# One table of places for every 4 and 8 KB buffer, whole 8 KB runs of expert weights, and a reordered last pair of experts

## The chip, the cores and the metric

The kernel runs on 1 core of one Trainium2 chip. The metric is the device time in microseconds. Before the change it is 823.57 us, the median of 3 runs (818.97 to 824.45). The profiled execution took 820.36 us, of which the span of recorded instructions is 818.6 us; all rows below are of that one execution. From run to run the kernel moves by about 0.7%, so a change of less than 1% can hardly be told from none here.

## The reference

One layer over 256 latent tokens of width 1024, with 256 context tokens, all in fp32. Cut to what matters:

```python
sh1, sc1, g1, sh2, sc2, g2 = split(silu(c) @ w_mod + b_mod, 6)      # and the same for the context
h, hc = modulate(x, sh1, sc1), modulate(ctx, sh1c, sc1c)
u, q, k, v, gates = split(h @ w_in);  uc, _, kc, vc, _ = split(hc @ w_in)
y_ssm = s5_both_directions(u, states left by uc)                    # scan of 64 states per group
o     = attention(rope(rms(q)), [rope(rms(k)), rms(kc)], [v, vc])   # 8 heads, 2 kv heads
g     = gelu(y_ssm)
mix   = (sig(gate_ssm) * (g @ w_glu_a) * sig(g @ w_glu_b) + sig(gate_attn) * (o @ w_attn_o)) @ w_out
x     = layer_norm(2**.25 * x + g1 * mix) * ln1_g + ln1_b
# 32 experts: best group of 4, best 2 of its 8 experts, for each token
y     = sum over chosen e of  w[t, e] * ((silu(m @ w_gate[e]) * (m @ w_up[e])) @ w_down[e]),  m = modulate(x, sh2, sc2)
x     = layer_norm(2**.25 * x + g2 * y) * ln2_g + ln2_b
```

The 32 experts' three matrices (gate and up 1024x512, down 512x1024) are 6 MB for an expert and 192 MB in all; every one is read once.

## The kernel before

**Two stages.** The first ("the flow", up to about 350 us) is everything up to the router. Its work is cut into some 45 small streams (Python generators), and a list of numbers, `Flow.ORDER`, says which stream emits its next piece; so the order of instructions on every engine is fixed when the kernel is built. The second stage loops over 16 pairs of experts (`for p in range(NP)`). Almost every instruction is recorded through one helper, line 238, so rows are told apart by tile names.

**A pair of experts.** Up to 64 tokens of each of two experts are gathered into one 128-wide operand. TensorE (PE) runs gate, 64-row products `gu<-ew,x` over eight k of 128 for both experts; after the first CB = 4 k of gate come eight products `acc<-yh,cw` and `acc<-yl,cw` that bring the pair before back to its tokens (`combine`). Then up, also eight k. ACT takes the silu of gate, DVE multiplies it with up into `hh`, PE transposes `hh` in between the gathering of the next pair (`dispatch`, `turn`), DVE copies it to `hT`, and the 32 products `y<-ew,hT` are down. In the last pair there is nothing to gather, so PE idles while `hh` and `hT` are made. The split of a result into two fp32r parts, `yh` (ACT) and `yl` (DVE), is what `combine` multiplies with `cw`.

**Buffers.** Large buffers come from several pools: `raw` (3 of 8 KB a partition), `p8` (5 of 8 KB), `p4` (15 of 4 KB), and `w`, `l4`, `g4` (4 of 4 KB each). The flow's own weights pass through `raw`, `l4`, `g4` and the rest. As the flow frees them, expert weights (`ew`) are loaded into them ahead of time (`prefetch8`, `prefetch4`, `refill`), and in the second stage the same buffers, 38 places of 4 KB as the list `first` has them, are used in a ring (`ring_tile`).

**Expert loads.** `eload` issues them on SP's queue. A buffer of 8 KB takes four k, one transfer of 1 MB in which each partition reads 8 KB in one run; a buffer of 4 KB takes two k, a transfer of 512 KB with runs of 4 KB. SP works its list in order: a transfer that waits for its buffer holds every later one. A transfer also waits, on one of eight semaphores (`DMAHW0` to `DMAHW7`) taken in turn, until the transfer eight before it has landed.

**Two pieces in the middle of the second stage.** `overflow()` handles tokens beyond 64 for an expert. It reads a count from memory on every engine (line 1709) and branches on it (line 1719); with these inputs there are none, so the body is skipped. It stands ahead of pair 8 (`OVP`). The last layer norm's gain and bias, one row of 1024 each, are spread over the partitions by four products of a 1-row operand, `y<-ew,count 1*128`, with an ACT copy each, in pair 14 ahead of up.

**Three transfers of the flow that the prediction speaks of.** `tm<-kscr` is eight loads of 128 KB on SP, of tables that PE reads as `ss<-tm,U`. `yT<-yscr` is one load of 512 KB that ACT issues on its own queue, in rows of 1 KB; ACT then works it into `gTh`, which PE reads in `acc<-wh,gTh`. `g<-in_w_mod` are loads of modulation weights in groups of four.

Of the kernel before, what the change touches and what calls it, by code (L numbers as in the profile page):

```python
# [31 lines left out]
NRAW = 3  # L32
N8, N4, N2, NPE = 5, 15, 6, 5
# [52 lines left out]
class Flow:  # L86
# [95 lines left out]
    def note(self, key, op, args, kw):  # L182
# [6 lines left out]
        for a in aps:  # L189
            assert a.tensor.name not in self.dead, (op, a.tensor.name)  # L190
# [1755 lines left out]
```

## Time and profile before

| | us |
|---|---|
| runs | 818.97, 823.57, 824.45 |
| profiled execution | 820.36 |
| its span | 818.6 |
| PE busy in the span | 765.9 (94%) |
| DVE busy | 371.6 (45%) |
| ACT busy | 295.3 (36%) |
| SP's DMA queue, share of the 16 engines' time | 83.7%, 265.29 MB |

PE's busy share is an average over two different stages. In the flow PE, DVE and ACT are all busy and the DMA engines between 45 and 93% (in stretches of 25 us). In the second stage DVE and ACT are at about a fifth, PE is at 100% of most 50 us stretches, and at the same time the DMA engines are at 1.02 of their time: two limits side by side. Times of rows are microseconds from the start of the span. A mean for one instruction is in ns. "idle before <-releaser" in brackets is how long the engine stood still ahead of a row and what ended that.

### The profile page before, as it was taken

Reading aid. Unit: us, or ns where it says so; the run is one execution under the profiler, and the core shown is the slowest. Engines: PE = TensorE matmul, PEld = TensorE weight load, DVE = VectorE, ACT = ScalarE, POOL = GpSimd, SP = SyncE. Lnnn points to the kernel's source line nnn. Section 1 sums busy time; section 2 is a strip of 40 time slices with the busy share of each in tenths; the row PEclk is TensorE's granted clock in tenths of the full one; section 3 lists DMA queues with packets and bytes.
Section 4 is the critical chain, followed back from the end, with each engine's and each line's share of the span. In section 5 each row is a group of like instructions: output and inputs, shape, how many; then the busy total and the mean of one; then the engine's idle time right before and its main releaser. Section 6 shows DMA issues by size and latency. Waiting matters only on the chain. (4 is left out here: it accounts for less than half of the span.)

```text
span 818.6 us, 11438 instructions
## 1 busy us (share of the span) xinstructions
PE 765.9 (94%) x4371; PEld 437.5 (53%) x4371; DVE 371.6 (45%) x857; ACT 295.3 (36%) x574; POOL 30.8 (4%) x48
## 2 busy tenths in 40 slices
PE   3999989989999999899999999999999999999994
PEld 1787777646667787644443444344344534444431
DVE  7999969877544767813211221122122122202115
ACT  5553586756988544522210221022022102202200
POOL 0004202000000000200000000000000000000000
PEclk9899999999999999899999999999999999999997
DMA  9977275593658686989999999999999999999992
GB/s 359 349 307 279 52 238 147 216 323 106 192 144 309 249 292 219 348 329 399 414 412 413 412 414 413 412 413 412 411 413 412 411 414 412 413 413 409 412 408 84
DMA packets 71138, 269.73 MB, mean 330 GB/s; under 512 B 12195, under 2 KB 17699, under 8 KB 59173
## 3 DMA queue, kind: packets, MB, share of 16 engines
q1 hardware_dynamic: 65268, 265.29, 83.7%
q0 software_dynamic: 1152, 2.59, 1.1%
q10 hardware_dynamic: 4656, 1.05, 0.6%
q8 instruction: 37, 0.61, 0.3%
q14 instruction: 25, 0.20, 0.1%
HBM read 265.79 MB, written 3.11 MB: 329 GB/s over the span
## 5 line engine op out<-in xcount | busy, mean ns | idle before, releaser
L238 PE MATMUL gu<-ew,x 128*64 128x512 f32 x1024 | 233.0, 602 | 4.4 <-PEq L1719 2.5
L238 PEld LDWEIGHTS gu<-ew,x 128*64 128x64 f32 x1024 | 75.3, 138 | 149.7 <-issue 134.5
L238 PE MATMUL y<-ew,hT 128*64 128x512 f32 x512 | 113.5, 595 | 0.8 <-DVE hT L238 0.8
L238 DVE TENSOR_TENSOR hh<-hh,gu 128x512 f32<-128x512 f32 x16 | 11.0, 688 | 212.1 <-PE gu L238 212.1
L238 ACT ACTIVATE x<-y,modT 128x128 f32<-128x128 f32 x120 | 45.1, 455 | 139.4 <-PE y L238 139.4
L238 DVE TENSOR_TENSOR wl<-raw,wh 128x1024 fp32r<-128x1024 f32 x52 | 63.4, 1223 | 28.7 <-ACT wh L238 28.5
L238 PEld LDWEIGHTS y<-ew,hT 128*64 128x64 f32 x512 | 36.3, 137 | 66.7 <-issue 63.6
L238 ACT ACTIVATE wh<-raw 128x1024 fp32r<-128x1024 f32 x52 | 54.9, 1059 | 25.2 <-PE acc L238 24.9
L238 PEld LDWEIGHTS y<-d,xh 128*128 128x128 f32 x480 | 55.9, 192 | 12.2 <-issue 10.5
L238 PE MATMUL acc<-wh,hh 128*128 128x512 f32 x128 | 57.3, 448 | 3.1 <-DVE q L238 2.0
L238 PE MATMUL y<-d,xh 128*128 128x128 f32 x480 | 60.0, 278 | 0.0
L238 ACT ACTIVATE yh<-x 128x512 fp32r<-128x512 f32 x32 | 20.1, 629 | 105.0 <-DVE x L238 105.0
L238 DVE SCALAR_TENSOR_TENSOR x<-y,wsl,g 128x512 f32<-128x512 f32 x32 | 24.0, 751 | 66.7 <-PE y L238 66.7
L238 ACT ACTIVATE hh<-gu 128x512 f32<-128x512 f32 x16 | 9.6, 597 | 123.4 <-PE gu L238 123.4
L238 PE MATMUL acc<-wh,hl 128*128 128x512 f32 x128 | 51.4, 401 | 0.0
L238 PE MATMUL acc<-wl,hh 128*128 128x512 f32 x128 | 51.3, 401 | 0.0
L238 DVE TENSOR_TENSOR yl<-x,yh 128x512 fp32r<-128x512 f32 x32 | 22.2, 692 | 24.1 <-ACT yh L238 24.1
L238 PEld LDWEIGHTS acc<-wh,hh 128*128 128x128 f32 x128 | 24.4, 190 | 11.8 <-issue 4.3
L238 PEld LDWEIGHTS acc<-wh,hl 128*128 128x128 f32 x128 | 24.5, 191 | 5.9
L238 PEld LDWEIGHTS acc<-wl,hh 128*128 128x128 f32 x128 | 24.5, 192 | 5.7 <-issue 1.2
L238 PE MATMUL acc<-yh,cw 128*128 128x512 f32 x64 | 27.0, 422 | 0.4 <-ACT yh L238 0.4
L238 PE MATMUL acc<-yl,cw 128*128 128x512 f32 x64 | 25.3, 395 | 0.2 <-DVE yl L238 0.2
(263 smaller groups left out, 1052.8 us busy)
## 6 DMA issues: line engine op xcount, KB each, us to landing
ew<-in_w_exp_gate_dram SPq DMA_DIRECT2D x92, 512.0 KB, 11.7
ew<-in_w_exp_up_dram SPq DMA_DIRECT2D x88, 512.0 KB, 11.4
ew<-in_w_exp_down_dram SPq DMA_DIRECT2D x84, 512.0 KB, 11.4
ew<-in_w_exp_down_dram SPq DMA_DIRECT2D x21, 1024.0 KB, 12.6
ew<-in_w_exp_up_dram SPq DMA_DIRECT2D x20, 1024.0 KB, 12.6
ew<-in_w_exp_gate_dram SPq DMA_DIRECT2D x18, 1024.0 KB, 12.5
g<-in_w_mod_dram SPq DMA_DIRECT2D x32, 512.0 KB, 6.7
raw<-in_w_in_dram SPq DMA_DIRECT2D x14, 1024.0 KB, 5.7
```

The source lines that it names most:

```text
L238: return f(*args, **kw)
```

## The change

**Places.** All the pools named above become one pool of 45 places of 4 KB, held as pairs (tiles `b0` to `b22`, 8 KB each but the last). Which place a buffer of the flow gets is read from a table, `Flow.PLACE`, in the order in which the buffers are made. The room for the two more places comes from `dynamic_dma_scratch_size=8192`. Rows of order show `b7_2709` where they showed `raw_2878` or `ew_2992`. `g2` now shares the place of `g1`.

**Expert loads.** `eload` now always loads four k, 1 MB in runs of 8 KB. The flow loads 18 of them where it loaded 16 MB, with a new stream `refill("x4", 4)`; twenty pairs of places (`units`) go round in the second stage. A pair is given back when all four k in it have been multiplied (`weight`), and `reload()` is called after gate, after up and after down.

**The last pair.** `overflow()` moves from pair 8 to the last pair, behind up. Three of the four products that spread the last norm's rows move from pair 14 into the last pair's up, behind six of its eight k (`UB` is 6, was 4); the fourth goes behind the last products of all. In the last pair `hh` is multiplied, transposed and copied in two halves of 256 columns. The second half of the last result is no longer split: two plain fp32 products take the place of four fp32r ones.

```diff
-    for n_, b_ in (("p8", N8), ("p4", N4), ("p2", N2), ("pe", NPE), ("t2", 2)):
+    for n_, b_ in (("p2", N2), ("pe", NPE), ("t2", 2)):
...
+    def places(self, at, n, dt=FT):
+
+        s, k = at // 2, FR if dt == FR else FT
+        if self.held.get(s, (None, None))[1] != k:
+            b = self.area.tile([P, min(2, NS - 2 * s) * W4], k, tag=f"b{s}", name=f"b{s}", bufs=1)
...
-                kn = 2 if small_ else 4
...
+        small_ = KINDS[tag][1] == 1
+        w, e, k0 = etiles[e_n[0]]
+        e_n[0] += 1
+        at = fl.at[fl.name(new(tag, [P, 2 if small_ else 4, F], name="ew"))]
+        if small_:
+            at = min(at, fl.at[fl.name(new(tag, [P, 2, F], name="ew"))])
+        r = fl.places(at, 2 * W4).rearrange("p (k c) -> p k c", c=F)
+        erun(r, w, e, k0, 4)
...
+    def reload():
+        while rest and units:
...
+    def weight(w, e, k):
+        u = where.pop((w, e, k))
+        left[u] -= 1
+        if not left[u]:
+            units.append(u)
+        return eready.pop((w, e, k))
...
-    NP, OVP, CB, UB = NE // 2, 8, 4, 4
+    NP, CB, UB = NE // 2, 4, 6
...
-        if p == OVP:
-            overflow()
...
         into(p, 1, range(UB))
+        if not more:
+            for i in range(3):
+                lnp = ln2_row(i, gu_p if i == 2 else y_p)
         into(p, 1, range(UB, KT))
...
+            overflow(lnp)
+            halves = [slice(256 * z, 256 * z + 256) for z in range(2)]
+            for c_ in halves:
+                tt(hh[:, c_], hh[:, c_], pgs[1][:, c_], OP.mult)
...
+            if more or n == 0:
+                split(yb[:, n], yh[n], yl[n])
+                if not more:
+                    combine(cw, (n,), True)
+            else:
+                for a in range(2):
+                    T.matmul(acc[a][n], cw[:, a].bitcast(FT), yb[:, n], start=False, stop=True)
+                ln2_row(3, gu_p)
```

In `ORDER` two entries 45 (the new stream) are put in and one 37 is moved.

**The order, first place: SP, the last two groups of `w_mod` loads** (about 166 to 175 us). Before:

```order
L238 DMA g4_1957<-in_w_mod_dram 128x1024 [waits DMAHW1_49,PE_49]
L238 DMA g4_1959<-in_w_mod_dram 128x1024 [waits DMAHW2_49,PE_49]
L238 DMA g4_1961<-in_w_mod_dram 128x1024 [waits DMAHW7_49,DMAHW3_49,PE_49]
L238 DMA g4_1963<-in_w_mod_dram 128x1024 [waits DMAHW4_49,DMAHW0_49,PE_49]
L238 DMA g4_2030<-in_w_mod_dram 128x1024 [waits DMAHW5_49,PE_49]
L238 DMA g4_2032<-in_w_mod_dram 128x1024 [waits DMAHW6_49,PE_49]
L238 DMA g4_2034<-in_w_mod_dram 128x1024 [waits DMAHW7_49,PE_49]
L238 DMA g4_2036<-in_w_mod_dram 128x1024 [waits DMAHW0_49,PE_49]
```

Now:

```order
L273 DMA b2_107<-in_w_mod_dram 128x1024 [waits DMAHW5_49]
L273 DMA b13_882<-in_w_mod_dram 128x1024 [waits DMAHW1_49,PE_49]
L273 DMA b10_481<-in_w_mod_dram 128x1024 [waits DMAHW7_49,DMAHW2_49,PE_49]
L273 DMA b9_113<-in_w_mod_dram 128x1024 [waits DMAHW3_49,DMAHW0_49,PE_49]
L273 DMA b12_123<-in_w_mod_dram 128x1024 [waits DVE_49]
L273 DMA b2_107<-in_w_mod_dram 128x1024 [waits DMAHW5_49,PE_49]
L273 DMA b13_882<-in_w_mod_dram 128x1024 [waits DMAHW6_49,PE_49]
L273 DMA b10_481<-in_w_mod_dram 128x1024 [waits DMAHW7_49,DMAHW4_49,PE_49]
```

The first load of each group no longer waits for PE's last use of its buffer.

**Second place: SP, from the `tm` loads to the second half of `w_glu_b`** (about 215 to 249 us). Before:

```order
L238 DMA raw_2538<-in_w_glu_b_dram 128x2048 [waits DMAHW6_49,DMAHW1_49,DVE_49]
L238 DMA ew_2592<-in_w_exp_gate_dram 128x2048 [waits DMAHW2_49]
L238 DMA tm_2601<-kscr_92 16x16x128 [waits DMAHW3_49,Activation_49]
L238 DMA tm_2601<-kscr_92 16x16x128 x2
L238 DMA tm_2601<-kscr_92 16x16x128 [waits DMAHW7_49]
L238 DMA tm_2601<-kscr_92 16x16x128 [waits DMAHW0_49]
L238 DMA tm_2601<-kscr_92 16x16x128 [waits DMAHW1_49]
L238 DMA tm_2601<-kscr_92 16x16x128 [waits DMAHW2_49]
L238 DMA tm_2601<-kscr_92 16x16x128 [waits DMAHW3_49]
L238 DMA ew_2690<-in_w_exp_gate_dram 128x2048 [waits DMAHW4_49,PE_49,Activation_49]
L238 DMA raw_2755<-in_w_glu_a_dram 128x2048 [waits DMAHW5_49,DVE_49]
L238 DMA raw_2878<-in_w_glu_b_dram 128x2048 [waits DMAHW0_49,DVE_49]
```

Now:

```order
L273 DMA b0_1347<-in_w_exp_gate_dram 128x2048 [waits DMAHW6_49,DMAHW2_49,DVE_49]
L273 DMA b21_1165<-kscr_89 16x16x128 [waits DMAHW3_49,PE_49]
L273 DMA b21_1165<-kscr_89 16x16x128 [waits DMAHW5_49]
L273 DMA b21_1165<-kscr_89 16x16x128
L273 DMA b21_1165<-kscr_89 16x16x128 [waits DMAHW7_49]
L273 DMA b21_1165<-kscr_89 16x16x128 [waits DMAHW0_49]
L273 DMA b21_1165<-kscr_89 16x16x128 [waits DMAHW1_49]
L273 DMA b21_1165<-kscr_89 16x16x128 [waits DMAHW2_49]
L273 DMA b21_1165<-kscr_89 16x16x128 [waits DMAHW3_49]
L273 DMA b1_115<-in_w_exp_gate_dram 128x2048 [waits DMAHW4_49,PE_49,Activation_49]
L273 DMA b11_337<-in_w_glu_a_dram 128x2048 [waits DMAHW5_49,PE_49]
L273 DMA b7_2709<-in_w_glu_b_dram 128x2048 [waits DMAHW7_49,DVE_49,PE_49]
```

The first `tm` load now waits for PE, which reads the older `tm` in the same place, where it waited for ACT. The `w_glu_b` load waits for a product of PE (of a `wh` in `b7`) where it waited for a DVE split. Three small loads and three expert loads of 1 MB follow it, where six of 512 KB did.

**Third place: PE, the end of the last pair's up.** Before, from its last products on:

```order
L238 MATMUL gu<-ew,x_3166 64x512 [waits DMAHW5_49]
L238 MATMUL gu<-ew,x_3166 64x512 x2
L238 MATMUL gu<-cst,hh 128x128 [waits DVE_49]
L238 MATMUL gu<-cst,hh 128x128 x3
L238 MATMUL y<-ew,hT 64x512 [waits DMAHW6_49,DVE_49]
```

Now, from the first use of the last two up transfers on (`b7` and `b8`):

```order
L273 MATMUL gu<-b_2709,b_452 64x512 [waits DMAHW3_49]
L273 MATMUL gu<-b_1212,b_452 64x512 [waits DMAHW4_49]
L273 MATMUL gu<-b_2709,b_452 64x512
L273 MATMUL gu<-b_1212,b_452 64x512
L273 MATMUL y<-b_1347,count 128x512 [waits PE_49] x2
L273 MATMUL gu<-b_1347,count 128x512 [waits Activation_49]
L273 MATMUL gu<-b_2709,b_452 64x512
L273 MATMUL gu<-b_1212,b_452 64x512
L273 MATMUL gu<-b_2709,b_452 64x512
L273 MATMUL gu<-b_1212,b_452 64x512
L1759 TENSOR_LOAD total [waits DVE_49]
L1769 COMPARE_AND_BRANCH
```

The three row products and the branch stand behind the wait for the last up transfers; the two transposes of each half follow the branch.

## Rows read from the trace of the kernel before

**Rows 1.** Windows of 50 us; last column GB/s, before it DMA share, granted clock.

```profile
400.00:450.00 50.00, 50.00 (x249) 20.91 (x250) 10.18 (x18) 8.22 (x18) 0.00 (x0) 1.00 1.02 413
700.00:750.00 50.00, 48.67 (x246) 23.03 (x243) 11.56 (x20) 9.13 (x21) 0.00 (x0) 1.00 1.02 411
```

**Rows 2.** Timeline of PE: start, length, what, idle before.

```profile
407.60 3.60 PE L238 MATMUL gu<-ew,x 128*64 128x512 f32 x16
...
574.60 5.35 PE L238 MATMUL gu<-ew,x 128*64 128x512 f32 x16 [2.52 <-PEq L1719]
...
685.81 3.60 PE L238 MATMUL gu<-ew,x 128*64 128x512 f32 x16
...
754.11 3.79 PE L238 MATMUL y<-ew,count 1*128 1x512 f32 x8
757.82 8.78 PE L238 MATMUL gu<-ew,x 128*64 128x512 f32 x32
...
777.88 3.60 PE L238 MATMUL gu<-ew,x 128*64 128x512 f32 x16
...
783.46 10.72 PE L238 MATMUL gu<-ew,x 128*64 128x512 f32 x48
...
796.47 7.24 PE L238 MATMUL y<-ew,hT 128*64 128x512 f32 x32 [0.79 <-DVE hT L238]
```

**Rows 3.** A window of 4 us behind the branch; granted clock third from the end.

```profile
574.00:578.00 4.00, 3.40 (x9) 1.23 (x11) 0.35 (x1) 0.00 (x0) 0.00 (x0) 0.59 1.01 416
```

**Rows 4.** Window at the end of the load stream.

```profile
801.00:802.00 1.00, 1.00 (x7) 0.66 (x5) 0.32 (x1) 0.63 (x1) 0.00 (x0) 1.00 0.08 31
```

**Rows 5.** Gate's expert loads on the page: count, KB each, us to landing.

```profile
ew<-in_w_exp_gate_dram SPq DMA_DIRECT2D x92, 512.0 KB, 11.7
...
ew<-in_w_exp_gate_dram SPq DMA_DIRECT2D x18, 1024.0 KB, 12.5
```

**Rows 6.** DMA view of three windows: 648:656, 456:460 and 552:556.

```profile
DMA packets 899, 3.28 MB, mean 410 GB/s; under 512 B 99, under 2 KB 99, under 8 KB 899
...
DMA packets 245, 1.69 MB, mean 422 GB/s; under 512 B 28, under 2 KB 28, under 8 KB 50
...
DMA packets 257, 1.71 MB, mean 427 GB/s; under 512 B 29, under 2 KB 29, under 8 KB 68
```

**Rows 7.** Timeline of ACT and DVE behind the last down product.

```profile
804.59 0.63 ACT L238 ACTIVATE yh<-x 128x512 fp32r<-128x512 f32 x1 [2.95 <-DVE x L238]
805.26 0.69 DVE L238 TENSOR_TENSOR yl<-x,yh 128x512 fp32r<-128x512 f32 x1 [0.76 <-ACT yh L238]
```

**Rows 8.** PE's waits, 160 to 200 us: total, times, longest.

```profile
PE ss L238 <- DMA g<-in_w_mod_dram: 3.4, 5, 1.1
```

**Rows 9.** Timelines of SP, PE and ACT around the `tm` and `yT` loads.

```profile
218.25 5.27 SPq L238 DMA_DIRECT2D tm<-kscr  x8
...
224.92 0.43 PE L238 MATMUL ss<-tm,U 128*32 128x128 f32 x8
...
233.71 0.43 PE L238 MATMUL ss<-tm,U 128*32 128x128 f32 x8
...
248.53 0.33 SPq L238 DMA_DIRECT2D raw<-in_w_glu_b_dram  x1
...
253.21 1.06 ACT L238 ACTIVATE gTh<-yT 128x1024 fp32r<-128x1024 f32 x1
...
255.62 0.48 PE L238 MATMUL acc<-wh,gTh 128*128 128x512 f32 x1
```

**Rows 10.** Loads on other queues: `tm` and `yT`, `kscr` at 70:82, `kscr` at 95:102.

```profile
DMA to landing us min/median/max: 4.9/5.1/5.3
...
yT<-yscr ACTq DMA_DIRECT2D x1, 512.0 KB, 4.0
...
kscr<-kall POOLq DMA_DIRECT2D x4, 32.0 KB, 5.7
...
kscr<-kall POOLq DMA_DIRECT2D x4, 32.0 KB, 2.1
```

More of the change, by code (lines that the diff above doesn't have):

```diff
@@ L254, in start @@
         aps = aps or ()
-        if any(a.tensor.name not in self.done for a in aps):
+        if any(self.name(a) not in self.done for a in aps):
             return None
@@ L1310, in flow_tile, with erun, eplace @@
-    def flow_tile(tag, shape):
-        return new(tag, shape, name="ew")
+    EW = ("w_exp_gate", "w_exp_up", "w_exp_down")
+    etiles = [(w, e, k0) for p in range(2) for w in EW for k0 in (0, 4) for e in (2 * p, 2 * p + 1)][:18]
+    eready, where, left, e_n = {}, {}, {}, [0]
+    def erun(o, w, e, k0, kn):
+        SY.dma_start(o.rearrange("p k c -> p (k c)"),
+             bass.AP(tensor=I[w].tensor, offset=I[w].offset + (e * P * 8 + k0) * F, ap=[[8 * F, P], [1, kn * F]]))
+    def eplace(o, w, e, k0, kn, at):
+        for k in range(kn):
+            eready[w, e, k0 + k] = o[:, k]
+            where[w, e, k0 + k] = at // 2
+        left[at // 2] = left.get(at // 2, 0) + kn
@@ L1323, in prefetch8 @@
     def prefetch8():
-        for _ in range(N8 - 3):
-            yield ask("Z", None, None, lambda: e_n[0] >= 4 and room("p8", 1)(), p8=1)
-            eload("p8", flow_tile)
+        for _ in range(2):
+            yield ask("Z", None, None, lambda: e_n[0] >= 2 and room("p8", 1)(), p8=1)
+            eload("p8")
         yield ask("Z", None, None, room("p8", 1), p8=1)
@@ L1352, in prefetch4 @@
     def prefetch4():
-        for i in range((N4 - 4) // 2):
+        for i in range(5):
             yield ask("Z", None, None, room("p4", 2), p4=2)
-            eload("p4", flow_tile)
+            eload("p4")
             if i == 2:
@@ L1618, in chunks @@
         while len(out_) < n:
-            tag = first[ring_n[0] % len(first)]
-            ring_n[0] += 1
-            m = 1 if small_(tag) else 2
-            r = ring_tile(tag, [P, m, D])
-            out_ += [r[:, z] for z in range(m)]
-        return out_
+            r = unit(D)[1]
+            out_ += [r[:, z] for z in range(2)]
+        return out_[:n]
     def weights():
@@ L1716, in overflow @@
         y = y.rearrange("p (n c) -> p n c", n=2)
-        pg = [gu_p.tile([P, F], FT, name="gu") for _ in range(2)]
-        yp = [y_p.tile([P, 512], FT, name="y") for _ in range(2)]
+        hh = t2[:, 8 * CAP:]
+        yp = pg = [y_p.tile([P, F], FT, name="y") for _ in range(2)]
         with tc.If(rv > 0):
@@ L1798, in into, with ln2_row @@
             for e in range(2):
-                T.matmul(pgs[i][64 * e:64 * e + 64], xgb[:, k, 64 * e:64 * e + 64], eready.pop((w, 2 * p + e, k)),
+                T.matmul(pgs[i][64 * e:64 * e + 64], xgb[:, k, 64 * e:64 * e + 64], weight(w, 2 * p + e, k),
                          start=(k == 0), stop=(k == KT - 1), tile_position=(0, 64 * e))
-    RING = sum(1 if small_(t_) else 2 for t_ in first)
+    def ln2_row(i, pool_):
+        row = eready["ln2", i // 2][:, F * (i % 2):F * (i % 2) + F]
+        ps = pool_.tile([P, F], FT, name="y" if pool_ is y_p else "gu")
+        T.matmul(ps, count[0:1, 0], row[0:1], start=True, stop=True)
+        S.activation(row, ps, AF.Copy)
+        return ps
+    reload()
     for p in range(NP):
@@ L1829, in build @@
             weighted(p + 1)
[L1830 to L1836 removed]
         into(p, 1, range(UB))
+        if not more:
+            for i in range(3):
+                lnp = ln2_row(i, gu_p if i == 2 else y_p)
         into(p, 1, range(UB, KT))
[L1839 to L1840 removed]
+        reload()
         hT = hTb
```

168 lines of the change are left out of this document (87 added, 81 removed).

## The prediction

> **What bounds the kernel now.** I read the 50 us windows first, then PE's timeline of the second stage, then the DMA view, and last the waits in the flow. The windows show two limits at once: from 400 us on PE is busy in 50.00 or 48.67 of 50 us, and the DMA engines are at 1.02 of their time with 411 to 413 GB/s [rows 1]. So each limit gets its own sum, and the later one counts.
>
> PE's chain: the first gate products of pairs stand at 407.60 and, ten pairs later, at 685.81 [rows 2]. Of these 278.2 us one pair had the branch: 2.52 us idle, and then 16 products in 5.35 us where other pairs need 3.60, together 4.3 us. The rest is 27.4 us a pair. From 685.81 to 777.88, three pairs, it is 92.1 us, 9.9 more than 3 x 27.4. Of that 3.8 us are the eight one-row products, and the 32 up products behind them took 8.78 us, 1.6 more than two thirds of the 10.72 that 48 of them took in the last pair [rows 2]. The remaining 4.5 us are late weights and small differences.
>
> The load stream: a pair's weights are 12 MB, 12.58 million bytes, which at 412.5 GB/s take 30.5 us. That is more than PE's 27.4, so what was loaded ahead is eaten up pair by pair. The last byte comes just ahead of 802, where the DMA share has fallen to 0.08 [rows 4], while PE is still in its last 32 products, from 796.47 for 7.24 us [rows 2]. Hence PE without its 14 us of losses would have run into the stream: what the stream gives is the question.
>
> **The change, part by part.**
>
> *Longer runs.* Gate's loads are 92 of 512 KB and 18 of 1 MB [rows 5], 28% of the bytes in 8 KB runs; up and down are alike. A window with no packet of 8 KB moved 410 GB/s, two that are nearly all 8 KB moved 422 and 427 [rows 6]. From the mean, 412.5 = 1/(0.72/410 + 0.28/x), x is 419. I take 420, near the low end, as the long stretch has more bytes than windows of 4 us. The stream is full from about 386 on, and the last up transfer lands the last 4 MB earlier than 802, at 802 - 10.2 = 791.8. Those 406 us become shorter by 1 - 412.5/420 = 1.8%, which is 7.2 us. Bounds: 0 (410, no gain) to 14 (427).
>
> The Trainium skill, "DMA: Bandwidth & Descriptors", section "Why small descriptors are slow", speaks against so much: it names three cycles of 32 bytes and 32 bytes of metadata a descriptor and finds merging worth it only at 256 bytes or less. By that, as an estimate, 8 KB runs are some 1.5% better than 4 KB ones, 1.0% of the mixed stream, 4.1 us, and the sum below would be 3.1 us worse. The rows show 3 to 4%, so I hold to them.
>
> *A megabyte more goes round*, 20 where there were 19: the stream is ahead by one transfer, 2.5 us at 412.5 GB/s. A place now comes free after four k instead of two, which can take back 1.8 us (16 products of 3.60 us are four k, half of it two). I take 2.5; bounds 0.7 and 2.5.
>
> So the last up transfer lands at 791.8 - 7.2 - 2.5 = **782.1**.
>
> *PE's chain to the same point.* Pair 15's gate would start at 777.88 - 4.3 (branch) - 5.4 (rows and slow products behind them) - 4.5 (late weights) = 763.7, and the fifth k of up, which needs the last up transfers, is 3.6 + 2.0 (combine: 783.46 - 777.88 - 3.6) + 3.6 + 3.6 = 12.8 later: 776.5 [rows 2]. So PE waits for the stream, about 5.6 us spread over the last pairs; most of what the branch and the rows cost in the middle is not gained, since those 14 us were covered by a stream that was late anyway.
>
> *Behind the last up transfer* all is on the path: 16 products 3.6, the three rows moved there 2.8 (three quarters of 3.79), the branch 2.5 (its idle time at pair 8), transposes and copies in halves, of which about 0.8 is not under the branch, and 32 products 7.1. Together 16.8, so the last down product ends at 798.9. Before it ended at 803.7: **-4.8**. The down transfers land until 782.1 + 10.0 = 792.1 and are in time. On DVE and ACT the branch comes long before `hh` is wanted; it costs nothing while they idle there, and 5 to 6 us if they were late.
>
> *The last result unsplit.* ACT's 0.63 and DVE's 0.69 us [rows 7] leave the path, and two plain products replace four: **-1.4**, bounds -1.6 and -0.5. The fourth row's product and copy are used only at the end of the first half's norm, several us later, and lie beside DVE's work.
>
> *The flow.* Three terms.
> First, the `w_mod` loads: PE waited 3.4 us for them in five places [rows 8], always for a late one of four; two of three groups now start one load early. I take -2.0, bounds -3.4 and 0.
> Second, `tm`: its first load was issued at 218.25, and must now wait for the end of the last reading of the older table, 224.92 + 0.43; that is 7.1 us later. The eight took 5.27 us to issue and 5.1 to land [rows 9, 10], so the last comes at about 235.4 or, if the landing is shorter with an emptier queue, 233.6. PE wants it at 233.71. I take +1.0, bounds 0 and 1.7.
> Third, `yT`: it landed in 4.0 us with its queue's engines to itself, as `w_glu_b` was issued only at 248.53 [rows 9, 10]. Now `w_glu_b` waits for a PE product that ends some 2 us earlier, so 1 MB, two small transfers and three more MB run beside it. A load on another queue does suffer: the 32 KB ones took 5.7 us beside a full queue and 2.1 in an empty one [rows 10]. `gTh` was ready at 253.21 + 1.06 = 254.27, and PE took it at 255.62, so 1.35 us are free. I take a delay of 2.3, +1.0 net; bounds 0 and the third rival's 8.6.
> The flow's sum is 0. A slip of it moves PE and stream alike, since the ring is refilled as pair 0 frees places.
>
> The sum: -4.8 - 1.4 + 0 = **-6.2 us**. The profiled execution of 820.36 becomes 814.2. It lies 3.2 under the median of the runs, so the median becomes 823.57 - 6.2 = **817.4**. Changes of 1% (815.3 and 831.8) are about what a measurement here tells from none.
>
> **Rivals.**
>
> 1. *The stream is no limit any more* (chance 0.25). At 427 GB/s the last up transfer lands at 791.8 - 13.8 - 2.5 = 775.5, before PE's 776.5. Then the down products end at 776.5 + 16.8 = 793.3, -10.4, with the tail -11.8, and 811.8; with the `w_mod` gain in full and no slip, 809. For it: the two windows of 422 and 427. Against it: both are 4 us long.
>
> 2. *Runs of 8 KB give next to nothing* (0.13). The stream gains only the megabyte, the last up transfer lands at 789.3, the down products end at 806.1, and with the tail it is +1.0: 824.6. Against it: [rows 6]. By the page of the Trainium skill named above, 4.1 us of the 7.2 would come and the time be 820.5, between this and the forecast.
>
> 3. *The flow slips, and the kernel is slower* (0.13). The two queues take turns, one packet each. `yT` is 512 rows of 1 KB, 32 on each of 16 engines; if each waits for a run of 8 KB, 8192 x 16 bytes at 422 GB/s or 0.31 us, it takes 9.9 us longer, 8.6 over what is free. PE standing still so long may also be followed by a lower clock, as the window after the branch shows 0.59, near the lower of 1.2 and 2.4 GHz [rows 3], which cost 1.75 us there. That makes 823.57 - 6.2 - 1.0 + 8.6 + 1.75 = 826.7. It decides from a slip of 6 us on. For it: the 32 KB loads. Against it: the small transfers behind `w_glu_b` have rows of 1 KB too and let `yT` through quickly.
>
> The rest, 0.49, is the forecast; inside it the clock may fall after the branch as it did in pair 8, +1.75, so 819.2.
>
> **How the numbers follow.** Faster by over 1% is rival 1 and a small part of the forecast: 0.32. Slower by over 1% needs rival 3 with something beside it, or a stall that no row shows: 0.09. The rest, 0.59, is within 1%. The likeliest time is 817.4. The range reaches to rival 1 without its full flow gain, 810.5, and up to rivals 2 and 3 in part, 825.5.
>
> **What would show it.** In the new profile: windows of 50 us at 419 to 422 GB/s with DMA share above 1; PE's `gu` waiting for expert loads in the last four or five pairs, 4 to 7 us in all; no idle time at pair 8 and no one-row products in pair 14; last-pair up products broken by a wait, then three rows, then about 2.5 us idle named after the branch; the first down product at about 791.5; about 1.4 us less from there on. In the flow, no waits for `g<-in_w_mod`, `tm` landing at 234 to 235, `yT` in 6 us or so. The forecast is wrong if the windows show 412 or 427, if `yT` takes 10 us, or if PE is late in the flow for a reason that none of these terms has.

## The result

| | before | after |
|---|---|---|
| median, us | 822.13 (818.97 to 824.45, 4 runs) | 810.05 (808.71 to 813.46, 4 runs) |
| ratio of times, with 95% interval | | 0.9867 (0.9844 to 0.9890) |
| profiled execution, its span | 820.36, 818.6 | 813.46, 811.6 |
| start of the second pair's gate, from the span's start | 380.16 | 379.70 |
| from there to the span's end ("second stage" below) | 438.4 | 431.9 |

Faster by 1.3%, where 0.75% was forecast. The profiled execution took 813.46; the forecast for it was 814.2. The four runs spread over 4.8 us, and the profiled one is the slowest of them. The unaltered change was timed twice more, beside other kernels, at ratios of 0.9921 (0.9899 to 0.9944) and 0.9890 (0.9863 to 0.9917). The mean of the three is 0.989, some 8.8 us.

**The load stream.** Windows of 50 us of the profile after, with the columns of [rows 1]:

```profile
400.00:450.00 50.00, 50.00 (x249) 20.57 (x247) 10.18 (x18) 8.23 (x18) 0.00 (x0) 1.00 1.01 421
700.00:750.00 50.00, 49.86 (x244) 21.27 (x242) 10.21 (x19) 8.70 (x20) 0.00 (x0) 1.00 1.01 421
```

DMA share is above 1 as before, and the stream moves 421 GB/s in place of 413 and 411. The page lists the gate loads in one form now, 64 of 1 MB, in place of the two of [rows 5]:

```profile
b<-in_w_exp_gate_dram SPq DMA_DIRECT2D x64, 1024.0 KB, 19.8
```

**PE in the last two pairs.** Timeline of PE of the profile after; it answers to [rows 2]:

```profile
736.73 3.65 PE L273 MATMUL gu<-b,b 128*64 128x512 f32 x16
...
742.34 7.98 PE L273 MATMUL gu<-b,b 128*64 128x512 f32 x34
751.64 3.65 PE L273 MATMUL gu<-b,b 128*64 128x512 f32 x14 [1.32 <-DMA b<-in_w_exp_up_dram]
...
766.56 3.64 PE L273 MATMUL gu<-b,b 128*64 128x512 f32 x16
...
772.17 7.97 PE L273 MATMUL gu<-b,b 128*64 128x512 f32 x34
781.45 1.93 PE L273 MATMUL gu<-b,b 128*64 128x512 f32 x6 [1.31 <-DMA b<-in_w_exp_up_dram]
783.31 1.98 PE L273 MATMUL y<-b,count 1*128 1x512 f32 x4
785.13 1.31 PE L273 MATMUL gu<-b,count 1*128 1x512 f32 x2
786.38 3.29 PE L273 MATMUL gu<-b,b 128*64 128x512 f32 x8
790.35 0.41 PE L273 MATMUL y<-cst,hh 128*128 128x128 f32 x2 [0.69 <-DVE hh L273]
790.68 0.41 PE L273 MATMUL gu<-cst,hh 128*128 128x128 f32 x2
791.32 7.09 PE L273 MATMUL y<-b,hT 128*64 128x512 f32 x32 [0.23 <-issue]
```

PE waits for an up transfer in pair 14 and in pair 15, 1.3 us each time; the view of waits has 2.6 us in two places for 350 to 815. That is less than PE loses. One of these products takes 0.59 us, and the next one starts some 0.21 us after it; so PE's row shows a stall only from the end of the product that is still running, and a short stall not at all. PE's weight loads (PEld) do not overlap in that way. Their view of waits, from 380 us on:

```profile
PEld gu L273 <- DMA b<-in_w_exp_up_dram: 6.8, 5, 2.2
```

The five places lie in pairs 13, 14 and 15, and some 0.3 us of each is the usual gap between weight loads. The pair times agree: from gate to gate pairs 2 to 12 take 27.36 or 27.37 us, pair 13 takes 28.58 and pair 14 29.83 (736.73 to 766.56), so 1.2 and 2.5 us are lost; in pair 15 another 2.1 are, since the 34 products ahead of 781.45 take 9.28 us where an unbroken row of them takes 7.18 (48 take 10.52). Together PE loses 5.8 us to the stream.

The first down product is at 791.32 (forecast 791.5), the last ends at 798.41 (forecast 798.9; before 803.71). The branch causes no idle time: behind it PE waits 0.69 us for DVE's `hh`. But the last eight up products, behind the three rows, took 3.29 us. The window there, granted clock third from the end:

```profile
785.00:790.00 5.00, 4.66 (x11) 0.95 (x9) 0.21 (x1) 1.26 (x3) 0.00 (x0) 0.66 0.82 318
```

0.66 over 5 us is a stretch partly at the lower of the two levels, 1.2 GHz, after the six one-row products; in the 3.3 us of the eight products alone it is 0.58.

**The tail.** Timeline of DVE of the profile after, behind the last down product:

```profile
798.46 0.75 DVE L273 SCALAR_TENSOR_TENSOR b<-y,wsl,b 128x512 f32<-128x512 f32 x1 [1.24 <-PE y L273]
799.12 2.00 DVE L273 BATCH_NORM_STATS2 fst<-acc 128x6 f32<-128x512 f32 x3
```

The ACT and DVE steps of [rows 7] are gone from this place. From the end of the last scaling to the end of the statistics it is 1.91 us (801.12 - 799.21), where it was 3.26 (807.76 - 804.50) in these rows of before:

```profile
803.75 0.75 DVE L238 SCALAR_TENSOR_TENSOR x<-y,wsl,g 128x512 f32<-128x512 f32 x1 [1.38 <-PE y L238]
...
805.87 1.89 DVE L238 BATCH_NORM_STATS2 fst<-acc 128x6 f32<-128x512 f32 x3
```

**The flow.** PE's waits in 160 to 200 us of the profile after (it answers to [rows 8]):

```profile
PE ss L273 <- DMA b<-in_w_mod_dram: 2.3, 3, 1.1
```

The timelines of SP, PE and ACT that answer to [rows 9]; `tm` and `yT` are called `b` too:

```profile
222.45 6.06 SPq L273 DMA_DIRECT2D b<-kscr  x8
...
232.46 0.86 PE L273 MATMUL ss<-b,b 128*32 128x128 f32 x24 [1.66 <-DMA b<-kscr]
...
244.69 0.37 ACTq L273 DMA_DIRECT2D b<-yscr  x1
...
245.12 0.33 SPq L273 DMA_DIRECT2D b<-in_w_glu_b_dram  x1
```

And the landing of `yT` in the DMA view of 240:250, as in [rows 10]:

```profile
b<-yscr ACTq DMA_DIRECT2D x1, 512.0 KB, 4.0
```

`w_glu_b` is issued 0.43 us behind `yT`, and `yT` lands in 4.0 us all the same. PE waits 1.66 us for `tm`. Between ACT's table loads at 154.65 and 185.77 before lay 31.1 us, in which [rows 8] lie; now they are at 156.48 and 184.60, 28.1 us apart.

### The profile page after: what moved, and what is told of

It reads as the page before. It is cut to its first block, busy times and chain, and to the rows that moved or that the text cites. A ratio compares the mean times of both kernels' runs of the same rounds, so it can differ in the third digit from the quotient of the medians.

```text
span 811.6 us, 11217 instructions
## 1 busy us (share of the span) xinstructions
PE 762.1 (94%) x4371; PEld 435.6 (54%) x4371; DVE 370.8 (46%) x858; ACT 294.2 (36%) x573; POOL 30.9 (4%) x48
## 5 line engine op out<-in xcount | busy, mean ns | idle before, releaser
L273 PE MATMUL gu<-b,b 128*64 128x512 f32 x1024 | 231.0, 597 | 3.4 <-DMA b<-in_w_exp_up_dram 2.6
L273 PE MATMUL acc<-b,b 128*128 128x512 f32 (+1 forms) x792 | 202.4, 390 | 4.4 <-DVE q L273 2.0
L273 PEld LDWEIGHTS acc<-b,b 128*128 128x128 f32 x792 | 136.5, 190 | 36.2 <-issue 9.2
L273 PEld LDWEIGHTS gu<-b,b 128*64 128x64 f32 x1024 | 73.3, 137 | 148.3 <-issue 138.6
L273 PE MATMUL y<-b,hT 128*64 128x512 f32 x512 | 113.4, 595 | 0.2 <-issue 0.2
L273 ACT ACTIVATE b<-y,modT 128x128 f32<-128x128 f32 x120 | 45.2, 456 | 138.5 <-PE y L273 138.5
L273 DVE TENSOR_TENSOR b<-b,b 128x1024 fp32r<-128x1024 f32 (+1 forms) x61 | 72.0, 1187 | 30.8 <-ACT b L273 29.7
L273 ACT ACTIVATE b<-b 128x1024 fp32r<-128x1024 f32 (+3 forms) x70 | 71.3, 1028 | 26.5 <-PE acc L273 24.2
L273 PEld LDWEIGHTS y<-d,b 128*128 128x128 f32 x480 | 55.9, 192 | 12.2 <-issue 11.4
L273 PE MATMUL y<-d,b 128*128 128x128 f32 x480 | 60.0, 278 | 0.0
L273 ACT ACTIVATE yh<-b 128x512 fp32r<-128x512 f32 x31 | 19.5, 629 | 97.5 <-DVE b L273 97.5
```

The lines of the kernel that those rows point to most:

```text
L273: return f(*args, **kw)
```

## The experiments

All times below of a "second stage" run from the second pair's gate to the span's end of the one profiled execution; "PE's wait" is the sum of waits for up transfers in PE's rows, "weight loads" the same in the rows of PEld, which also show the short ones (with some 0.3 us of usual gap in each). The stage is the finer gauge: three profiles of the unaltered change have 431.9, 431.6 and 431.8, two of before 438.4 and 438.7, while the start of the stage moves between 377.1 and 382.6 from run to run in kernels whose flow is the same.

| kernel | median, us | ratio (95%) | second stage | PE's wait | weight loads |
|---|---|---|---|---|---|
| again | 813.63 | 0.9921 (0.9899 to 0.9944) | 431.6 | 2.6 | 6.6 |
| run4k | 823.51 | 1.0040 (1.0022 to 1.0057) | 443.4 | 7.6 | 20.9 |
| ring19 | 815.33 | 0.9937 (0.9912 to 0.9962) | 432.2 | 4.2 | 9.2 |
| half64 | 1175.08 | (not given) | 790.8 | 97.5 | (not used) |
| nobranch | 815.31 | 0.9906 (0.9873 to 0.9939) | 431.5 | 3.4 | 7.9 |
| rows14 | 812.91 | 0.9883 (0.9851 to 0.9914) | 431.5 | 0 | 1.7 |
| both | 815.01 | 0.9918 (0.9890 to 0.9946) | 434.2 | 0 | 0.7 |
| resplit | 814.64 | 0.9910 (0.9879 to 0.9940) | 433.8 | 2.6 | 6.6 |
| again2 | 812.92 | 0.9890 (0.9863 to 0.9917) | 431.8 | 2.6 | 6.9 |
| rows14nb | 809.81 | 0.9843 (0.9814 to 0.9872) | 428.5 | 1.0 | 2.8 |
| rowsmid | 810.23 | 0.9866 (0.9834 to 0.9898) | 430.7 | 1.6 | 4.5 |

The lines from again to half64 ran on one chip, from nobranch to resplit on another, the last three on a third. The kernel before had 820.63, 821.67 and 821.90 there.

### The longer runs: run4k, half64, and the change again

**again**: the change, unaltered.

> The changed kernel unaltered, for a second trace and a closer ratio. The forecast put the change at -6.2 us (ratio 0.9925); the first timing said 0.987, -11 us, while its one profiled execution was -6.9 us against the one of before. If the forecast's sum is right for the second stage and the profiled execution merely began badly, this trace has the second stage as in the first one (last up products behind a wait for the stream of 1 to 3 us, last down product near 8 us ahead of the DVE end) and differs in the flow, by 2 to 5 us: PE's waits for w_mod in the first 60 us near 0.8 instead of 2.7, a half-speed stretch more or less. The rival: the second stage itself varies by 3 to 5 us.

Measured: 813.63 against 820.63. Its profile repeats that of the change to 0.3 us from the second gate on; its flow is 2.6 us shorter (gate at 377.06). Of these 1.8 lie where it was expected: PE's waits for `w_mod` in the first 60 us are 0.9, where the change's first profile has 2.7.

**run4k**: two k a transfer everywhere, 4 KB runs, all else as changed.

```diff
-            n = 1 if w == "w_exp_down" and k0 and e == NE - 1 else 4
+            n = 1 if w == "w_exp_down" and k0 and e == NE - 1 else 2
```

> The changed kernel with each 1 MB transfer of the second stage issued as two of 512 KB with runs of 4 KB a partition, same places and order; the 18 transfers of the flow stay as they are. Stream theory (8 KB runs shorten a stream that sets the end): 50 us windows fall from 420 to 410 GB/s, PE's waits for expert loads grow from 2.6 to about 10 us, time +7 to +10 us, ratio to before 0.995 to 1.0. Rival (the stream is no limit; the moved pieces made the gain): windows fall too, but the time stays within 2 us of the changed kernel, ratio 0.985 to 0.989.

Measured: 9.9 us slower than again, and 0.4% slower than before. A 50 us window of run4k:

```profile
450.00:500.00 50.00, 50.00 (x264) 22.82 (x264) 10.97 (x20) 9.73 (x22) 0.00 (x0) 1.00 1.03 409
```

Its DMA view of 600:620:

```profile
DMA packets 2240, 8.17 MB, mean 408 GB/s; under 512 B 249, under 2 KB 249, under 8 KB 2239
```

And that of the same stretch of the profile after:

```profile
DMA packets 1156, 8.43 MB, mean 422 GB/s; under 512 B 128, under 2 KB 128, under 8 KB 128
```

At a full DMA share 409 became 421 GB/s, 2.9%. Of the some 406 us in which the stream is full that is nearly 12 us; the second stage differs by 443.4 - 431.6 = 11.8. So the rate sets the time nearly one for one, which it could not if the stream were no limit. The pair times show how: in both kernels a pair takes 27.4 us while the loads that went ahead last; from pair 11 on run4k's pairs take 29.1 to 31.7 us, where again has 28.4 and 29.8 in pairs 13 and 14 only. run4k is also 5.0 us longer in the second stage than before the change. But it has no 8 KB runs there, where 28% of the expert bytes had them before: at 409 in place of 412.5 GB/s the 406 us become some 3.5 longer. So the run shows that the rest of the change gains nothing without the faster stream; that it would lose with the old mix of runs is not shown.

**half64**: 8 KB runs in transfers of 512 KB, each of 64 partitions, to part the run's length from the transfer's size.

```diff
-                erun(r[:, k:k + n], w, e, k0 + k, n)
+                for h in (0, 64) if n == 4 else ():
+                    SY.dma_start(r[h:h + 64].rearrange("p k c -> p (k c)"),
+                         bass.AP(..., offset=I[w].offset + ((e * P + h) * 8 + k0) * F, ap=[[8 * F, 64], [1, 4 * F]]))
```

> The changed kernel with each 1 MB transfer of the second stage issued as two of 512 KB, 64 partitions each, runs of 8 KB kept. If the length of the run makes the rate, windows stay at 420 GB/s and the time within 2 us of the changed kernel. If it is the size of the transfer, windows fall to 410 to 412 and the time grows by 7 to 10 us.

Measured: 1175.08 us. It did not part the two, since transfers of half as many partitions moved nearly half as much. A 50 us window of half64, and its DMA view of 600:620:

```profile
600.00:650.00 50.00, 36.06 (x130) 14.36 (x132) 4.34 (x8) 3.96 (x10) 0.00 (x0) 0.83 1.02 227
```

```profile
DMA packets 688, 4.51 MB, mean 225 GB/s; under 512 B 139, under 2 KB 139, under 8 KB 139
```

The DMA share is 1.02, the rate 227 GB/s. Whether the run's 8 KB or the transfer's 1 MB gives the 2.9% stays open: in all other kernels here the two change together.

### One place less: ring19

```diff
+    spare = units.pop()
```

> The changed kernel with one pair of places fewer in the second stage (19 go round, as many bytes as before the change). Stream theory: the stream is one transfer less ahead, 2.5 us later at the last up products, so +2.5 us (1 to 3). Rival (the extra megabyte is not needed, PE sets the end): 0 to +0.5 us.

Measured: the wait in the last pair's up ends 403.61 us after the second gate (780.91 - 377.30); in again it is 401.58 (778.64 - 377.06). One megabyte in the ring is worth 2.0 us there, where the forecast took 2.5. By the rows of PE's weight loads the waits grew by 2.6 us. The second stage lost only 0.6, which is close to what the rival had foreseen (0 to 0.5), but for another reason: the eight products behind the rows ran at the full clock this time, 1.94 us at a granted clock of 1.00, and not 3.41 as in again. The median is 1.7 us higher. PE of ring19:

```profile
780.91 1.93 PE L273 MATMUL gu<-b,b 128*64 128x512 f32 x6 [1.31 <-DMA b<-in_w_exp_up_dram]
...
785.54 1.94 PE L273 MATMUL gu<-b,b 128*64 128x512 f32 x8
```

### The branch and the rows: nobranch, rows14, both, rows14nb, rowsmid

**nobranch**

```diff
-            overflow(lnp)
```

> The changed kernel without the handling of overflowing tokens in the last pair (none overflow with these inputs; the body and its branch are left out). The forecast charged 2.5 us of idle time to the branch there: by it, the first down product comes 2.5 us sooner after the last up transfers and the time falls by 2.5 us (ratio 0.989 where the unaltered changed kernel had 0.9921). The trace of the changed kernel shows only 0.7 us of idle time there, put down to DVE's hh: by that rival the branch is covered by products still queued on PE and the time stays within 0.7 us.

Measured: second stage 431.5, as with the branch. In its timeline the idle time ahead of the transposes is the same 0.69 us:

```profile
789.85 1.94 PE L273 MATMUL gu<-b,b 128*64 128x512 f32 x8
792.48 0.41 PE L273 MATMUL y<-cst,hh 128*128 128x128 f32 x2 [0.69 <-DVE hh L273]
```

So the branch behind up cost nothing in the change. Yet its eight products took 1.94 us and not 3.29, so it should have won 1.4 us; that it didn't is because its wait ended 402.66 us after the second gate (785.22 - 382.56), 0.9 later than in the change; why it did is open.

**rows14**: the rows (all four) back in pair 14, the branch left behind the last up.

```diff
-        if p == NE // 2 - 2:
+        if p == NE // 2 - 3:
...
+        if p == NP - 2:
+            for i in range(4):
+                ln2_row(i, y_p)
         into(p, 1, range(UB))
-        if not more:
-            for i in range(3):
-                lnp = ln2_row(i, gu_p if i == 2 else y_p)
```

> The changed kernel with the four one-row products of the last norm back in pair 14 ahead of up, as before the change (their weights loaded one pair sooner). Stream theory: in pair 14 they take 3.8 us and leave a slower clock behind, 5 us in all, of which the waits for the stream in pairs 14 and 15 (1.3 us each in the changed kernel) take back 2.6; in the last pair 3 us of rows and about 1.4 us of slow products vanish from behind the last up transfers. Net -1 to -2.5 us, no wait for the stream left in pair 15. Rival (PE's work is the limit everywhere, so its place does not matter): within 0.5 us.

Measured: no gain in the second stage. PE's rows show no wait for the stream any more (its weight loads 1.7 us in place of 6.8), but the branch shows. PE of rows14:

```profile
774.01 11.51 PE L273 MATMUL gu<-b,b 128*64 128x512 f32 x48
788.76 0.41 PE L273 MATMUL y<-cst,hh 128*128 128x128 f32 x2 [3.24 <-PEq L1769]
...
789.74 8.60 PE L273 MATMUL y<-b,hT 128*64 128x512 f32 x32 [0.35 <-issue]
```

The branch on its PE sequencer, by the view of the line (duration in ns three times, then its start):

```profile
L1769 PEldq COMPARE_BRANCH  x1: 5912/5912/5912, 782.5 to 782.5; - x1
```

The same row of the profile after:

```profile
L1769 PEldq COMPARE_BRANCH  x1: 6106/6106/6106, 782.1 to 782.1; - x1
```

Both hold the sequencer for 6 us. In rows14 it begins with 3.0 us of products still queued on PE (785.52 - 782.5), so 3.24 us are idle, and down follows in 8.60 us in place of 7.09. In the change it begins at 782.1 with the rest of the six, the six row products and the last eight queued, 7.6 us of work (789.67 - 782.1), and is hidden. The slow one-row products are a good part of what hides it.

**both**: rows14, and the branch ahead of the last up.

```diff
+            overflow(gu_p.tile([P, F], FT, name="gu"))
+        into(p, 1, range(UB))
...
-            overflow(lnp)
```

> rows14, and the overflow branch moved ahead of the last pair's up, where PE waits for the stream anyway. If the branch costs 2.5 us at the end, this is 1.5 to 2.5 us faster than rows14. If it is covered at the end, moving it gains nothing, and it may lose up to 2.5 us as PE stands still ahead of up without the queue of products that covers it now.

Measured: 434.2. The branch is as bare there as in rows14:

```profile
747.39 4.21 PE L273 MATMUL y<-b,count 1*128 1x512 f32 x8
751.53 10.01 PE L273 MATMUL gu<-b,b 128*64 128x512 f32 x32
...
785.40 8.44 PE L273 MATMUL gu<-b,b 128*64 128x512 f32 x32 [3.36 <-PEq L1769]
```

But the branch's place is not what makes it 2.7 us longer than rows14. The first two rows lie in pair 14, which is the same in both kernels: the 32 products behind the one-row products took 10.01 us at a granted clock of 0.56 (750 to 755 us), and 7.09 at 1.00 in rows14. From the last pair's gate to the span's end both takes 42.9 us (815.7 - 772.81) and rows14 43.1 (811.5 - 768.43). So moving the branch ahead of up neither won nor lost.

**rows14nb**: rows14 without the branch.

```diff
-            overflow(gu_p.tile([P, F], FT, name="gu"))
```

> rows14 (row products back in pair 14) without the overflow branch, which these inputs never take. In rows14 PE stood idle 3.2 us behind the branch; with the rows in the last pair it did not. If the rows, queued on PE behind the last up transfers, are what covers the 6 us of the branch, then leaving both away from there shows their joint price: the second stage from pair 1's first gate product to the end takes 427 to 428.5 us instead of 431.5, ratio 0.983 to 0.986. If the branch had another cover, it stays at 431 to 432.

Measured: 428.5, 3.0 less than rows14 and 3.3 less than again2, which was timed beside it, with a ratio of 0.9843. So rows and branch together cost the second stage 3.3 us in the last pair. The rows alone cost 3.0 (nobranch against this), the branch alone 3.0 (rows14 against this), and the two together no more than one, as they lie over each other. The price of the rows is the less certain one: 0.9 us of it is nobranch's late wait, which is unexplained.

**rowsmid**: the three rows and the branch between the last gate and the last up, where PE would wait for the stream anyway.

```diff
-        into(p, 1, range(UB))
         if not more:
             for i in range(3):
                 lnp = ln2_row(i, gu_p if i == 2 else y_p)
+            overflow(lnp)
+        into(p, 1, range(UB))
```

> The changed kernel with the three row products and the branch moved from behind six k of the last pair's up to ahead of up, where 1.3 us of waiting for the stream follow. If the stream's last up transfers set the time there, 2.8 us of rows go from behind that wait to ahead of it and the wait goes: -1 to -2 us, unless the branch is uncovered there (only gate products and rows are queued ahead of it, and up behind it), which would give back 1 to 3 us. Rival (place does not matter): within 0.5 us; second stage 431.5.

Measured: 430.7, 1.1 less than again2; the median is 2.7 us lower, with intervals that overlap. PE of rowsmid:

```profile
774.45 1.98 PE L273 MATMUL y<-b,count 1*128 1x512 f32 x4
776.27 1.02 PE L273 MATMUL gu<-b,count 1*128 1x512 f32 x2
777.94 8.78 PE L273 MATMUL gu<-b,b 128*64 128x512 f32 x32 [0.65 <-ACT b L273]
```

The branch, from 771.6 to 777.6, is covered by the last 16 gate products (to 774.52) and the rows, but for the 0.65 us ahead of up, which the profile puts down to ACT. The 32 products behind the rows took 8.78 us, as long as the 32 behind them in pair 14 before [rows 2]. Of the versions in the table that still handle overflowing tokens it has the lowest median and the shortest stage, though by less than the timing can settle.

### The unsplit tail: resplit

```diff
-            if more or n == 0:
+            if True:
```

> The changed kernel with the second half of the last result split and combined by four fp32r products again, as before the change. The forecast's term of 1.4 us: time +1.4 us, the first statistics of the norm 3.3 us behind the end of the last down product instead of 1.9. Rival (the two plain fp32 products cost as much as the split): within 0.4 us.

Measured: second stage 433.8, 2.0 more. DVE of resplit:

```profile
797.69 0.75 DVE L273 SCALAR_TENSOR_TENSOR b<-y,wsl,b 128x512 f32<-128x512 f32 x1 [1.26 <-PE y L273]
799.20 0.69 DVE L273 TENSOR_TENSOR yl<-b,yh 128x512 fp32r<-128x512 f32 x1 [0.76 <-ACT yh L273]
799.81 1.89 DVE L273 BATCH_NORM_STATS2 fst<-acc 128x6 f32<-128x512 f32 x3
```

From the end of the last scaling to the end of the statistics it is 801.70 - 798.44 = 3.26 us; in the change 801.12 - 799.21 = 1.91. The term is 1.35 (forecast 1.4). The rest of the 2.0 is not the tail but the clock: its eight products behind the rows took 2.64 us and its 32 down products 8.74 (granted 0.77 from 787.6 to 797.6), where again2 has 3.40 and 7.09.

### The runs themselves: again2, before2

**again2** is the change once more, **before2** the kernel before, profiled a second time.

> The changed kernel unaltered once more. Two timings gave ratios of 0.9867 and 0.9921, whose intervals do not meet; the forecast was 0.9925. If the spread between timings comes from the flow's run to run differences (pair 1 began between 377.1 and 382.6 us in the traces so far that share this flow), this ratio falls between 0.986 and 0.993, and the second stage from pair 1's first gate product to the end is 431.5 us again, within 0.5.

> The kernel before, unaltered, for a second trace: where pair 1 begins (380.16 us in the first) and how long the second stage takes from there (438.4). If runs differ in the flow only, the second is 438.4 again within 0.5 and the first moves by up to 3 us.

Measured: 431.8 and 438.7 in the second stage, with second gates at 379.10 and 381.30. In before2 the 32 products behind the one-row products of pair 14 took 7.12 us at the full clock, and not 8.78 as in [rows 2], yet its second stage is no shorter: its weight loads wait 8.1 us for up transfers, where those of the first trace wait 5.8. What PE gains in the middle, it waits for later. before2 puts 30.6 us between the two table loads of ACT (156.14 and 186.78), again2 28.7 and again 27.7. Of the twelve profiles with the changed flow ten have 27.7 to 29.5, two have 30.4 and 31.9.

## Why the prediction was right or wrong

**Right: two limits, and what the stream gives.** 420 GB/s forecast, 421 measured; the last wait for an up transfer forecast to end at 782.1, measured 781.45; the first down product at 791.5 and 791.32. Against the shift of the whole stage by -0.46 (379.70 - 380.16), the down products end 4.84 us sooner, forecast 4.8, and the tail gives 1.35, forecast 1.4. Over all profiles the second stage is 6.8 us shorter (438.6 to 431.8), where the two terms made 6.2; 0.3 of the rest is the last store, which ends 3.0 us behind DVE in place of 3.3.

**Right: PE's chain up to there.** Pair 15's gate began at 766.56. Without the 1.2 and 2.5 us lost to the stream in pairs 13 and 14, and without the shift, that is 766.56 - 3.7 + 0.46 = 763.3, forecast 763.7. PE lost 5.8 us to the stream, forecast about 5.6, though in three pairs and not in four or five.

**Rivals 1 and 2 fall.** The stream still ends last: PE waits for it in the last three pairs, and run4k and ring19 move its last wait by nearly what they take away. And 8 KB runs in transfers of 1 MB do give something: 2.9% against 4 KB runs in transfers of 512 KB. The Trainium skill, "DMA: Bandwidth & Descriptors", section "Why small descriptors are slow", gave some 1.5% as an estimate from its cycles and metadata. Its limit of 256 bytes is for joining consecutive descriptors into one packet, which is not what was changed here. run4k measured 409 and 421 GB/s at a full share, nearly twice the estimate, and for these two forms of loads the measurement decides. As run4k halved the transfers too, it is not shown that the runs alone give so much.

**Behind the last up transfer the sum was met by luck.** It was to be 16.8 us to the end of the last down product, and it was 16.96 (798.41 - 781.45), from pieces that cancelled. The branch was costed at 2.5 us of idle time, from its place in pair 8. It cost none, since its 6 us on the sequencer were covered by 7.6 us of queued products; the row of before showed the cover of another place. Against this, transposes and copies took 1.65 us from the last up product to the first down product (791.32 - 789.67), not 0.8; the rows took 3.07, not 2.8; and the up products 5.15, not 3.6, as the last eight took 3.29 in place of 1.94. The lower clock was expected after the branch's idle time and came after the one-row products.

**The step that failed: "The flow's sum is 0", and the median that it was added to.** Of the flow's three terms the first holds: the stretch with the `w_mod` loads became some 2 us shorter (28.9 on average of twelve, against 31.1 and 30.6), forecast -2.0; PE's waits for the loads, 1.9 on average against 3.4 and 2.8, are 1.2 of it. Its second holds: PE's waits for `tm` are 0.5 to 1.7 us in the twelve, 1.2 on average, forecast +1.0. Its third fails: the +1.0 for `yT` is 0, with a landing of 4.0 us, the same as with the engines to itself (3.9 to 4.2 in the nine profiles of the changed flow whose view shows it). **Rival 3** falls with it. So the flow's sum by its own terms is about -0.8, and the start of the second stage says -1.5: 380.7 on average of two profiles before, 379.2 of twelve after. With a spread of 5.5 us from run to run, two profiles before are too few to fix that figure. With the stage's -6.8 that is 7.6 to 8.3 us, of the 8.8 of the three timings. The other half of the step is "the median becomes 823.57 - 6.2". 823.57 is the median of three runs; with the fourth it is 822.13, and in the later timings it was 820.63 to 821.90.

**The miss, added up.** From 817.4 to 810.05 it is 7.3 us: 1.4 from the median of before, 0.8 from the flow's own terms, 0.6 from the second stage, 0.7 more by which the second stage starts earlier, and 3.8 by which this one timing lies beyond all that the profiles show. So the flow's failed term is only a small part of the miss, and the second stage, whose limits the forecast had right, is another small one.

**What the range lacked.** It was built from terms of one execution; but kernels with the same flow start their second stage anywhere in 377.1 to 382.6. That spread was named as the 0.7% between runs, but put at nothing in the range. The first timing's ratio, 0.9867, is the far one of three, and its median lies just beneath 810.5. Part of the spread goes with the granted clock that each run lists. Those four runs list 0.984 on average and took 810.6 us; the six of again 0.980 and 813.6; the six of again2 0.981 and 813.0. Of the 45 later runs of the kernel before, the 18 that list 0.976 or less took 823.1 us on average, and the 5 that list 0.982 or more 818.8. What sets that clock in one run and not in another no run here shows. Some of the flow's differences are visible (a stretch at the lower clock, a `w_mod` wait of up to 2.2 us), but their cause stays open too.

## What to carry to other kernels

Where DMA engines are at their full share, the form of the transfers is still a rate to be had: compare GB/s at the same share between windows with different runs before trusting a rule about what is too small. Before saying how long PE waited, compare the times of equal pieces of work, or look at its weight loads: PE's rows showed 2.6 us of a loss of 5.8. A branch's price is its time on the sequencer less the work queued ahead of it, so cost it at the new place, from the queue there. And judge a change of under 1% by the stage it touches, measured from an event within the run, and give the rest of the kernel its own spread.

## What the runs showed of the hardware

- **Loads to 64 partitions at half the rate.** Two transfers of 64 partitions with 8 KB runs moved 227 GB/s at a DMA share of 1.02; one of 128 moved 421 at 1.01. The Trainium skill, "DMA: Bandwidth & Descriptors", section "Rules for kernel authors", says of two transfers to disjoint partition halves not to bother, since they share the same engines; here it was not merely no gain but nearly half the rate.
- **A skipped body costs PE 6 us of its sequencer.** The same branch took 5.9 to 6.2 us on PE in every profile that has it but half64 (8.7), and 45 to 72 ns on DVE, ACT, SP and POOL in the change. The Trainium skill, "Runtime: NRT & Kernel Launch", section "Instruction fetch mechanics", says that a branch taken to a target outside the instructions at hand waits for them to be fetched; that fits a long body on PE, but no run here made the body shorter.
- **The lower clock comes and goes.** The eight products behind the rows took 1.94 us at a granted clock of 1.00 (nobranch, ring19), 2.62 to 2.69 (run4k, resplit, half64) or 3.29 to 3.41 at 0.54 to 0.58 (the change, again, again2), with the same instructions ahead of them. In pair 14 the 32 products behind the eight one-row products took 7.09 us (rows14, rows14nb), 7.12 (before2), 8.78 (before) or 10.01 (both).
- **A load on another queue need not suffer.** 512 KB on ACT's queue landed in 4.0 us with a transfer of 1 MB issued on SP's 0.43 us behind it, where [rows 10] had shown 5.7 against 2.1 us for small ones on POOL's. It was issued first; how it would fare behind such transfers no run here shows.
